# Where a DMA-bound kernel waits for its last store: ahead of the closing barriers, or behind them

## The chip, the cores and the metric

The kernel runs on one core of one Trainium2 chip. Times are device microseconds (us). The state of one core's executions can't be told from a second die, so a run counts as fast unless it lies over 1.5% above the fastest of its kernel; all timed runs here were fast, except one single run whose state is unknown and whose time is not used. PE (matrix products; PEld is its weight loading), ACT, DVE and POOL are the engines that compute; SP here only issues transfers and waits. A semaphore is a counter that instructions raise and wait for; in the traces each of the 23 DMA transfers raises its own by 16 in all, and "landed" here means that the sixteenth increment is there. A barrier is a point at which every engine waits until all have arrived. "Span" is the time from the first to the last instruction of the kernel's own program in the trace.

## The reference

```python
# x: 16 x 2048 x 256 float32;  W: 256 x 256;  rank 16;  scale = 1.0
x_flat = x.reshape(-1, 256)
y = x_flat @ W
lora_out = ((x_flat @ lora_A) * lora_E) @ lora_B
y = y + scale * lora_out        # 16 x 2048 x 256 float32
```

Input and output are 33.5 MB each. The kernel folds the low-rank part into one 256 x 256 weight matrix at the start, so that the rest is one matrix product over 32,768 rows.

## The kernel before

The rows are cut in 8 chunks of 4 MB. A chunk is loaded to SBUF, cast to bf16 by POOL, transposed by PE, copied by ACT, multiplied by PE, copied back over the loaded data by DVE, and stored. SP issues every load and store, in the fixed order below. All of this stands in one "critical block". At its end all engines signal SP once. The last store alone stands behind the block, so that the framework tracks it and waits for it when the kernel closes.

```python
ORDER = [
    "L0", "L1", "L2", "L3", "L4", "L5",
    "S0", "S1", "L6", "L7", "S2", "S3", "S4", "S5", "S6", "S7",
]
# ... (cut)
    stored_of = {c: sem(f"stored_{c}") for c in range(N_CHUNKS - N_HOMES)}   # chunks 0, 1
    stored_rest = sem("stored_rest")                                         # the others
# ... (cut) in the program of SP:
        for step in ORDER[:-1]:
            c = int(step[1:])
            if step[0] == "L":
                # ... (cut) loads
            else:
                sync.wait_ge(s_chunk, c + 1)
                # ... (cut)
                sync.dma_start(out=y_chunks[c], in_=home(c)[:]).then_inc(stored_of.get(c, stored_rest), 16)
# ... (cut)
    with tc.tile_critical(no_gpsimd_drain=True):
        sync_program()
        gpsimd_program()
        scalar_program()
        vector_program()
        tensor_program()

    last = int(ORDER[-1][1:])
    nc.sync.dma_start(out=y_chunks[last], in_=home(last)[:])
```

What the framework adds behind that last line is not in the source, but it is in the built program: SP waits for the last store; then come a drain, a barrier of all five engines, one POOL instruction that clears the kernel's semaphores, and a second barrier.

## Time and profile before

| | before |
|---|---|
| timed | 164.98 us, median of 3 runs (164.93 to 165.04) |
| span of the profiled run | 163.28 us |
| last PSUM copy of DVE ends | 122.27 us |
| last store issued | 122.66 us |
| last store landed (16th increment of its semaphore) | 162.30 us |
| closing work behind the landing | 0.99 us |

From the page of the kernel before: the span; busy time of each engine with its share of the span; the share of DMA by fortieths of the span, in tenths (9 is 90% or more); the queue of loads and stores with packets, MB and its share of 16 engines' span; and the bytes of HBM.

```profile
span 163.3 us, 2148 instructions
...
PE 99.2 (61%) x778; PEld 82.6 (51%) x778; DVE 79.6 (49%) x66; ACT 66.1 (40%) x65; POOL 67.1 (41%) x70
...
DMA  5999999998998998999999999999999999999990
...
q1 hardware_dynamic: 2976, 67.41, 96.8%
...
HBM read 33.85 MB, written 33.56 MB: 413 GB/s over the span
```

No compute engine is busy more than 61%, and the DMA queue 96.8%. The last digit of the DMA row is 0: in the last 4 us (159.2 to 163.3 us) the 16 engines move little. Two things are in there: fifteen of them finish and one is late, still moving bytes until 161.8 us (after 160.25 us the trace has one packet of 32 KB at a time in flight, the last one ending at 161.83 us), and then, for the last 1.45 us, nothing moves at all.

The timeline of the kernel before from 120 us, with start, duration, engine, line and operation; "SPq" is SP's issuing of a DMA:

```profile
119.69 2.57 DVE L181 COPY home<-psum_y 128x1024 f32<-128x1024 f32 x2 [0.24 <-PE psum_y L204]
...
122.66 0.33 SPq L241 DMA_DIRECT2D out_dram<-home  x1
```

The waits of the DMA queue in the kernel before: who waited, for what, us in total, how often, and the longest:

```profile
SPq L130 <- DVEq L185: 42.0, 4, 13.3
...
SPq L272 <- DMA out_dram<-home: 39.3, 1, 39.3
SPq L230 <- DVEq L230: 10.9, 1, 10.9
...
SPq L272 <- PEq L272: 0.7, 2, 0.6
```

Line 272 is the framework's closing code. SP sits there for 39.3 us after the last store is issued. Add 122.66 + 0.33 + 39.3 and you are at 162.3 us, 1 us before the end of the span. That last microsecond is what the change is after. The line of L230 is the wait at the end of the critical block, for DVE's last chunk. The last line is two waits for the other engines in the closing barriers, 0.7 us together.

The printed views leave out semaphore instructions, so here is what the trace records behind the landing, as a list of start (us), engine and instruction. Semaphores 96 and 97 are the two halves of the barrier, 133 is the one that counts the last store.

```
162.296  sixteenth increment of semaphore 133 arrives
162.313  SP    wait for 133 passes
162.372  SP    drain
162.435  SP    arrives at the first barrier
162.588  SP    released (the others by 162.650)
162.679  SP    arrives at the second barrier
162.762  POOL  clears semaphores 99 to 133, 0.225 us
163.099  POOL  has all arrivals of the second barrier
163.219  SP    released (PE, the last, ends at 163.282)
```

The sixteen increments of that last store did not come together: fifteen arrived between 159.38 and 160.59 us, the last at 162.30 us. In the trace, packets of this store follow each other back to back in chains of eight of 32 KB, 1.21 us each, with one of 4 bytes behind the eighth (so in the 11 chains that can be told apart from end to end); there are 16 of these 4-byte packets. The chain that ended last, at 161.83 us, was 1.6 us behind the next (160.24 us). With 16 engines on the page, the author reads a chain as one DMA engine's work and its 4-byte packet as one increment.

### The profile page before, as it was taken

What the parts mean: (1) busy time and instruction counts of PE and PEld (TensorE: products, weight loads), DVE (VectorE), ACT (ScalarE), POOL (GpSimd) and SP (SyncE); (2) the same over time, 40 slices, a digit from 0 to 9 for tenths busy, and PEclk for the clock granted to TensorE, in tenths of its full rate; (3) what the DMA queues carried; (4) which work ended last, traced back from release to release, by engine and by line L of the source; (5) the groups of instructions that cost most, each with busy time, mean ns of one, the idle gap of its engine ahead of it and who ended that gap; (6) DMA issues with size and microseconds to landing.
All of it is one profiled execution on the core that took longest, in us unless ns stands there. A gap on an engine that the chain in (4) does not pass through costs nothing. (4 is left out here: it accounts for less than half of the span.)

```text
span 163.3 us, 2148 instructions
## 1 busy us (share of the span) xinstructions
PE 99.2 (61%) x778; PEld 82.6 (51%) x778; DVE 79.6 (49%) x66; ACT 66.1 (40%) x65; POOL 67.1 (41%) x70
## 2 busy tenths in 40 slices
PE   0399948999999999999930089999960000000000
PEld 0268837888888888888820078888840000000000
DVE  0115861788988888888850025888880000000000
ACT  3044732777767676777720025677720000000000
POOL 1444615777777677777500155677500000000000
PEclk9999995999999999999995557999996555555555
DMA  5999999998998998999999999999999999999990
GB/s 165 411 452 458 393 498 393 409 490 385 466 433 385 490 385 379 417 425 468 409 442 433 409 450 425 427 433 442 417 450 409 450 425 433 442 425 433 450 393 16
DMA packets 2979, 67.43 MB, mean 413 GB/s; under 512 B 528, under 2 KB 544, under 8 KB 672
## 3 DMA queue, kind: packets, MB, share of 16 engines
q1 hardware_dynamic: 2976, 67.41, 96.8%
q14 instruction: 3, 0.02, 0.0%
HBM read 33.85 MB, written 33.56 MB: 413 GB/s over the span
## 5 line engine op out<-in xcount | busy, mean ns | idle before, releaser
L181 DVE COPY home<-psum_y 128x1024 f32<-128x1024 f32 x64 | 78.4, 1225 | 32.8 <-PE psum_y L204 30.0
L151 POOL CAST stage<-home 128x1024 bf16<-128x1024 f32 x64 | 66.4, 1041 | 48.8 <-PE psum_xt L196 24.8
L162 ACT COPY xt<-psum_xt 128x1024 bf16<-128x1024 bf16 x64 | 64.8, 1012 | 52.7 <-PE psum_xt L196 52.7
L204 PE MATMUL psum_y<-weff,xt 128*128 128x256 bf16 x512 | 70.2, 283 | 1.0
L204 PEld LDWEIGHTS psum_y<-weff,xt 128*128 128x128 bf16 x512 | 48.3, 101 | 14.7 <-issue 7.1
L196 PE MATMUL psum_xt<-ident,stage 128*128 128x128 f32 x260 | 42.6, 290 | 14.0 <-PEq L189 14.0
L196 PEld LDWEIGHTS psum_xt<-ident,stage 128*128 128x128 f32 x260 | 33.2, 151 | 16.1 <-issue 15.1
L216 PE MATMUL psum_y<-ident,a_sb 128*16 128x128 f32 x2 | 0.6, 396 | 6.8 <-DMA a_sb<-in_lora_A_dram 6.8
L167 DVE TENSOR_SCALAR ate<-psum_y,e_sb 16x256 f32<-16x256 f32 x1 | 0.5, 471 | 7.5 <-PE psum_y L216 7.5
L216 PEld LDWEIGHTS psum_y<-ident,a_sb 128*16 128x16 f32 x2 | 0.1, 90 | 6.8 <-issue 6.8
L222 PE MATMUL psum_y<-b_sb,ate 16*128 16x256 f32 x4 | 2.1, 666 | 0.0
L177 DVE TENSOR_TENSOR weff<-w_sb,psum_y 128x512 bf16<-128x512 f32 x1 | 0.7, 689 | 2.4 <-PE psum_y L222 2.4
L162 ACT ACT_TABLE_LOAD x1 | 1.3, 1283 | 0.9 <-SPq L230 0.9
L222 PEld LDWEIGHTS psum_y<-b_sb,ate 16*128 16x128 f32 x4 | 1.2, 318 | 0.5 <-issue 0.3
L133 POOL MEMSET ident<- 128x128 f32 x1 | 0.2, 204 | 0.5 <-SPq L230 0.5
L135 POOL TENSOR_SCALAR_AFFINE_SELECT ident<-ident 128x128 f32<-128x128 f32 x1 | 0.3, 293 | 0.2 <-POOL ident L133 0.2
L258 POOL MEMSET const-float32-0.0<- 128x1 f32 x1 | 0.1, 98 | 0.2 <-issue 0.2
L258 POOL MEMSET const-bfloat16-1.0<- 128x1 bf16 x1 | 0.1, 101 | 0.0
L258 POOL MEMSET const-uint8-127<- 128x1 uint8 x1 | 0.1, 101 | 0.0
L258 POOL MEMSET const-float32-1.0<- 128x1 f32 x1 | 0.1, 98 | 0.0
## 6 DMA issues: line engine op xcount, KB each, us to landing
out_dram<-home SPq DMA_DIRECT2D x8, 4096.0 KB, 42.1
home<-in_x_dram SPq DMA_DIRECT2D x7, 4096.0 KB, 19.9
home<-in_x_dram SPq DMA_DIRECT2D x2, 1024.0 KB, 5.3
home<-in_x_dram SPq DMA_DIRECT2D x1, 2048.0 KB, 10.1
w_sb<-in_W_dram SPq DMA_DIRECT2D x1, 256.0 KB, 5.1
a_sb<-in_lora_A_dram SPq DMA_DIRECT2D x1, 16.0 KB, 4.9
e_sb<-in_lora_E_dram SPq DMA_DIRECT2D x1, 0.1 KB, 4.6
b_sb<-in_lora_B_dram SPq DMA_DIRECT2D x1, 16.0 KB, 4.0
```

What stands on the lines that cost most here:

```text
L133: gpsimd.memset(ident[:], 0.0).then_inc(s_ident, 1)
L135: gpsimd.affine_select(out=ident[:], in_=ident[:], compare_op=ALU.not_equal, fill=1.0, base=0, pattern=[[-1, P]], channel_multiplier=1,).t ...
L151: gpsimd.tensor_copy(out=stage[g % NS][:], in_=home(c)[:, b:b + CG, :]).then_inc(s_stage, 1)
L162: scalar.copy(out=xt[g % NX][:], in_=halves).then_inc(s_xt, 1)
L167: vector.tensor_scalar(out=ate[:], in0=psum_y[0][:R, :KT, :P], scalar1=e_sb[:], scalar2=float(scale), op0=ALU.mult, op1=ALU.mult,).then_in ...
L177: vector.tensor_add(out=weff[:], in0=w_sb[:], in1=psum_y[1][:, :KT, :]).then_inc(s_free, NY)
L181: vector.tensor_copy(out=home(c)[:, b:b + CG, :], in_=psum_y[g % NY][:]).then_inc(s_free, 1)
L196: ins = tensor.transpose(psum_xt[i % NT][:, b, :], words[:, b, :], ident[:])
L204: ins = tensor.matmul(psum_y[i % NY][:, b, :], xt[i % NX][:, b, t, :], weff[:, t, :], start=(t == 0), stop=(t == KT - 1),)
L216: ins = tensor.transpose(psum_y[0][:R, t, :P], a_sb[:, t, :], ident[:])
L222: ins = tensor.matmul(psum_y[1][:, t, :], ate[:, t, :], b_sb[:], start=True, stop=True)
L258: nc = _bacc.Bacc("TRN2", target_bir_lowering=False, num_devices=1)
```

## The change

Its intent is to put the closing work under the stores that are still running. The last store is issued within the critical block, as the others are. No store is tracked by the framework any more, so the closing barriers don't wait for any. SP waits for all six open stores (96 increments) in one instruction, added after the framework's closing code. The semaphore must outlive POOL's clearing, which now runs while increments are still coming in. So it is taken from outside the framework's pool, and POOL clears two ranges, one on each side of it (99 to 114 and 116 to 132 in the trace; the stores' semaphore is 115).

```diff
-    stored_rest = sem("stored_rest")
+    stored_rest = nc.alloc_semaphore("stored_rest")
@@
-        for step in ORDER[:-1]:
+        for step in ORDER:
@@
-    last = int(ORDER[-1][1:])
-    nc.sync.dma_start(out=y_chunks[last], in_=home(last)[:])
+    def wait_for_stores(nc):
+        nc.sync.wait_ge(stored_rest, 16 * N_HOMES).then_inc(stored_rest, -16 * N_HOMES)
+
+    nc.at_finalize(wait_for_stores)
```

## The prediction

> **What bounds the kernel now.** The DMA, from end to end. On the page its queue is busy 96.8% of 16 engines' span (413 GB/s, 67.4 MB); PE, the busiest engine, 61%. Compute ends early: the timeline has DVE's last PSUM copy ending at 122.3 us of the 163.3 us span, and from there to about 159 us the windows view shows only DMA, at 426 to 442 GB/s. The trace's semaphore updates show the last four stores landing 9.7 us apart (133.3, 143.0, 152.6, 162.3 us), long after their issues.
>
> **The end of the span.** The last store is issued at 122.66 us (timeline; 0.33 us to issue). SP then waits 39.3 us for its landing (longest wait of the DMA queue, on the kernel's last line), to 162.31 us. Only then come a drain, an all-engine barrier, POOL's clearing of the semaphores (0.225 us) and a second barrier, to 163.28 us: 0.97 us of closing work behind the last byte, serial, on the path that ends last. [...] 15 increments come between 159.38 and 160.59 us, the sixteenth at 162.30 us. One slow engine sets the end; the change doesn't touch it.
>
> **What the change does.**
> 1. The last store moves ahead of the critical block's closing exchange (122.32 to 122.66 us in before), so it is issued about 0.3 us sooner. Worth nothing: stores are queued before it on the same engines.
> 2. The drain, both barriers and the clearing now run at about 122.5 to 123.7 us, under the DMA. POOL clears two ranges instead of one, since the stores' semaphore is kept out: hidden.
> 3. After them stands one SP wait. Such an instruction takes 0.017 us in the trace, so the span should end about 0.03 us after the landing instead of 0.97 us: 0.94 us saved.
> 4. The timed 164.98 us exceeds the span by 1.7 us. The trace shows updates of another semaphore from 163.52 to 164.04 us, after the kernel's end, which I take for the runtime's barrier [...]. Its third update comes 0.205 us after the second, where the opening one has 0.04 us: an engine came late. With four engines there 38 us ahead, it waits for SP alone. I estimate 0 to 0.3 us and count 0.15 us, if the timer covers it.
>
> **Sum.** 164.98 − 0.94 − 0.15 = 163.9 us, 0.7% faster: within 2%. Range 163.4 to 164.3 us. Chances: faster by over 2% 0.02, within 2% 0.96, slower by over 2% 0.02.
>
> **What would show it.** The last store is issued near 122.3 us on the stores' own line, and lands within 0.2 us of 162.3 us as before (1). Barriers and clearing show near 123 us, none after 160 us (2). The queue's last wait is for the stores, on the added line; the span ends within 0.05 us of it (3). The timed median falls by more than the span (4). DMA GB/s and busy times stay.
>
> **What would make it wrong.** The last DMA engine's lag (1.7 us behind the fifteenth) may differ between programs or chips; it enters one to one. The idle engines may fetch their closing instructions during the stores and take DMA time on the slow engine. The timer may leave out the closing barrier, or SP may reach it late: then 0.9 us or less is gained. Over 2% would need 3.3 us, more than everything after the landing.

That the updates from 163.52 to 164.04 us are a barrier of the runtime was the author's reading, and the 0.15 us an estimate from the two gaps (0.205 against 0.04 us). Of the risks: the traces do show packets on an instruction queue, but the three in the span of the kernel before (8 KB and 0.31 us each) came at 62.6, 73.5 and 102.7 us, those of the changed kernel at 59.4, 72.0 and 102.3 us, and none during the last stores.

## The result, and the profile after

| | before | after |
|---|---|---|
| timed, median | 164.95 us (4 runs, 164.81 to 165.04) | 163.59 us (4 runs, 163.36 to 163.85) |
| span of the profiled run | 163.28 us | 162.04 us |
| last store landed | 162.30 us | 162.00 us |
| from landing to end of span | 0.99 us | 0.03 us |
| timed minus span | 1.79 us (mean of 11 runs) | 1.35 us (mean of 4 runs) |

The ratio of the changed kernel to the kernel before is 0.9921, with a 95% interval of 0.9904 to 0.9938. Ratios here are those of fast runs of the same rounds, so they are not quite the ratio of the medians in the tables. The 1.79 us are from the first batch of experiments below, where each run of the kernel before lists its span.

The page of the changed kernel, the same lines as shown of before:

```profile
span 162.0 us, 2150 instructions
...
PE 96.9 (60%) x778; PEld 80.1 (49%) x778; DVE 79.6 (49%) x66; ACT 66.1 (41%) x65; POOL 67.1 (41%) x70
...
DMA  5999898999999997999999999999999999999992
...
q1 hardware_dynamic: 2976, 67.41, 97.5%
...
HBM read 33.85 MB, written 33.56 MB: 416 GB/s over the span
```

The same bytes are moved in the same number of packets. The share rose from 96.8% to 97.5% because the span is shorter. From 124 to 159 us, the stretch in which the stores alone run, the two kernels look the same (first before, then changed; busy time of PE, PEld, DVE, ACT and POOL, granted PE clock, DMA share, GB/s):

```profile
124.00:159.00 35.00, 0.00 (x0) 0.00 (x0) 0.00 (x0) 0.00 (x0) 0.00 (x0) 0.50 1.00 432
```

```profile
124.00:159.00 35.00, 0.00 (x0) 0.00 (x0) 0.00 (x0) 0.00 (x0) 0.00 (x0) 0.50 1.00 431
```

Timeline of the changed kernel from 120 us, then the waits of its DMA queue:

```profile
119.98 1.23 DVE L181 COPY home<-psum_y 128x1024 f32<-128x1024 f32 x1
121.28 0.33 SPq L130 DMA_DIRECT2D out_dram<-home  x1
```

```profile
SPq L130 <- DVEq L185: 50.5, 5, 13.3
...
SPq L238 <- SPq L238: 39.0, 1, 39.0
...
SPq L271 <- PEq L271: 0.9, 2, 0.7
```

The last store is now on line 130 with the others. The wait at the end of the critical block (10.9 us on line 230 before) is gone; line 130 has five waits instead of four, because SP now waits for DVE's last chunk there. The closing barriers (line 271) take 0.9 us. They run from 121.8 to 123.1 us, and nothing of them is left after 160 us. The 39.0 us wait on line 238 is the added one. The view names SP itself as what it waited for. That is an artefact: the instruction also subtracts 96 from the semaphore that it waits on, and this is the update that came last. The real releaser is the store, whose sixteenth increment arrived at 162.005 us; the wait passed at 162.021 us and ended the span at 162.038 us.

### The profile page after: what moved, and what is told of

Same layout as the page of the kernel before. It is cut to its first block, busy times and chain, and to the rows that moved or that the text cites. A ratio compares the mean times of both kernels' runs of the same rounds, so it can differ in the third digit from the quotient of the medians.

```text
span 162.0 us, 2150 instructions
## 1 busy us (share of the span) xinstructions
PE 96.9 (60%) x778; PEld 80.1 (49%) x778; DVE 79.6 (49%) x66; ACT 66.1 (41%) x65; POOL 67.1 (41%) x70
## 3 DMA queue, kind: packets, MB, share of 16 engines
q1 hardware_dynamic: 2976, 67.41, 97.5%
## 5 line engine op out<-in xcount | busy, mean ns | idle before, releaser
L204 PE MATMUL psum_y<-weff,xt 128*128 128x256 bf16 x512 | 68.4, 278 | 0.4
L204 PEld LDWEIGHTS psum_y<-weff,xt 128*128 128x128 bf16 x512 | 47.0, 99 | 14.4 <-issue 6.4
L196 PE MATMUL psum_xt<-ident,stage 128*128 128x128 f32 x260 | 41.1, 283 | 16.0 <-PEq L189 16.0
L196 PEld LDWEIGHTS psum_xt<-ident,stage 128*128 128x128 f32 x260 | 31.9, 147 | 18.1 <-issue 17.2
```

The lines of the kernel that those rows point to most:

```text
L196: ins = tensor.transpose(psum_xt[i % NT][:, b, :], words[:, b, :], ident[:])
L204: ins = tensor.matmul(psum_y[i % NY][:, b, :], xt[i % NX][:, b, t, :], weff[:, t, :], start=(t == 0), stop=(t == KT - 1),)
```

## The experiments

The theory to test, called the closing theory: the gain is the closing work that no longer follows the landing (0.95 us of span), plus a shorter wave of updates afterwards, taken for the runtime's barrier (timed minus span fell by 0.44 us). Rivals: the earlier issue of the last store makes the gain; barriers cost their time wherever they stand; the shorter time behind the span has another cause; the DMA was luckier in the later runs.

Two batches of four were run (r1 and r2 followed), each on one chip with runs of the kernel before beside it. In the first the kernel before took 165.12 us in the median (11 runs), in the second, on another chip, 164.62 us (11 runs). So compare within a batch, or compare ratios. This table has all eight. The landing is that of the one profiled run; "timed − span" is a mean over all timed runs, and is 1.79 us for the kernel before in both batches.

| run | ratio to before (95%) | landing | landing to end of span | timed − span |
|---|---|---|---|---|
| first batch: e0_after_again | 0.9921 (0.9896 to 0.9947) | 161.97 | 0.03 | 1.32 |
| e2_issued_behind_barriers | 0.9914 (0.9888 to 0.9941) | 162.28 | 0.03 | 1.32 |
| e5_barriers_ahead_of_wait | 0.9932 (0.9904 to 0.9961) | 162.99 | 0.03 | 1.34 |
| e6_all_engines_wait | 0.9958 (0.9930 to 0.9986) | 162.11 | 0.18 | 1.82 |
| second batch: e1_issue_moved_only | 1.0027 (1.0011 to 1.0042) | 161.74 | 1.43 | 1.75 |
| e3_issued_20us_later | 0.9925 (0.9911 to 0.9939) | 161.82 | 0.03 | 1.33 |
| e4_barriers_behind_stores | 1.0036 (1.0022 to 1.0051) | 161.77 | 1.30 | 1.79 |
| e7_act_waits | 0.9933 (0.9918 to 0.9947) | 161.83 | 0.04 | 1.46 |

### e0: the changed kernel again

No edit.

> The changed kernel again, as the reference of this batch. Closing theory (the 0.97 us of barriers and semaphore clearing no longer follow the last landing, and the runtime's barrier after the kernel needs only SP): 0.992 of the kernel before, about 163.6 us, with time minus span about 1.35 us against about 1.7 us before. If the first result was luck of the DMA, the ratio comes back nearer 1.

It took 163.69 us in the median of 6 runs, against 165.12 us, with the same ratio as at first. The gain is not luck. What was luck is that the store landed 0.3 us earlier in the first profile of the changed kernel than in that of the kernel before: in the means of all timed runs, listed to 0.1 us, the span of e0, e2, e3 and e7 is 0.81 to 0.89 us shorter than that of the kernel before, and not more than the 0.95 us of closing work. The tenth that is missing is within the noise (standard error 0.11 to 0.17 us).

### e1: only the issue is moved

```diff
-    stored_rest = nc.alloc_semaphore("stored_rest")
+    stored_rest = sem("stored_rest")
+        sync.wait_ge(stored_rest, 16 * N_HOMES)      # at the end of SP's part of the critical block
-    nc.at_finalize(wait_for_stores)                  # and the function with it
```

> The last store is issued inside the critical block as in the change, but SP waits for the stores there, ahead of all closing work. Closing theory: no gain; the critical block's closing exchange (0.40 us in the changed kernel's trace) now also follows the landing, so 0.3 to 0.4 us slower than the kernel before, about 165.3 us. Rival (earlier issue): the gain stays, about 163.6 us.

It took 164.95 us against 164.62 us before. The profile has the store's issue as early as in the changed kernel:

```profile
121.18 0.33 SPq L130 DMA_DIRECT2D out_dram<-home  x1
```

The view of the DMA queue's waits books the wait for it, 40.2 us, on line 106, together with the two waits before the last two loads:

```profile
SPq L106 <- DMA out_dram<-home: 82.1, 3, 40.2
```

So an early issue alone gains nothing, and this half of the change alone even loses: 1.43 us stand behind the landing instead of 0.99 us, because the signals at the end of the critical block now follow the landing too. The ratio of 1.0027 is 0.44 us of 164.62, and 1.43 − 0.99 is 0.44 us.

### e2: the issue moved the other way

```diff
-        for step in ORDER:
+        for step in ORDER[:-1]:
     def wait_for_stores(nc):
+        nc.sync.dma_start(out=y_chunks[last], in_=home(last)[:]).then_inc(stored_rest, 16)
         nc.sync.wait_ge(stored_rest, 16 * N_HOMES).then_inc(stored_rest, -16 * N_HOMES)
```

> The last store is issued behind the closing barriers, about 1.7 us later than in the changed kernel and later than in the kernel before; the final wait stays last. Closing theory: same as the changed kernel, within 0.2 us, since three stores (29 us of DMA) are queued before it. Rival (the gain comes from the earlier issue of the last store): the gain is gone, 165 us or more.

```profile
122.94 0.33 SPq L240 DMA_DIRECT2D out_dram<-home  x1
```

```profile
SPq L241 <- SPq L241: 39.0, 1, 39.0
```

The store is issued later than in the kernel before (122.66 us), and the whole gain is there: 163.57 us, against 163.69 us of the changed kernel in the same batch. The intervals of the two ratios overlap nearly in full.

### e3: the last store issued 20 us later

The sixth chunk's store gets a semaphore of its own, `stored_5`, and the last store is issued only when that one has landed:

```diff
     def wait_for_stores(nc):
+        nc.sync.wait_ge(stored_5, 16).then_inc(stored_5, -16)
+        nc.sync.dma_start(out=y_chunks[last], in_=home(last)[:]).then_inc(stored_rest, 16)
-        nc.sync.wait_ge(stored_rest, 16 * N_HOMES).then_inc(stored_rest, -16 * N_HOMES)
+        nc.sync.wait_ge(stored_rest, 16 * (N_HOMES - 1)).then_inc(stored_rest, -16 * (N_HOMES - 1))
# ... (cut) the new semaphore, its use by the sixth store, and the loop over ORDER[:-1]
```

> The last store is issued only once the sixth chunk's store has landed, near 143 us, some 20 us later than in the change; one whole store is still queued before it. Closing theory: same as the changed kernel within 0.3 us, about 163.6 us. Rival (issue time counts): 165 us or more.

The timeline and the two long waits of this run:

```profile
142.56 0.33 SPq L242 DMA_DIRECT2D out_dram<-home  x1
```

```profile
SPq L241 <- SPq L241: 20.3, 1, 20.3
SPq L243 <- SPq L243: 19.0, 1, 19.0
```

SP slept 20.3 us before the issue and 19.0 us after it, and the ratio is 0.9925. With one 4 MB store still queued (9.7 us of DMA), it didn't matter here that the next was issued 20 us later. The rival of the earlier issue is out.

### e4 and e5: four more barriers, behind the final wait or ahead of it

```diff
     def wait_for_stores(nc):
+        # e5: here
         nc.sync.wait_ge(stored_rest, 16 * N_HOMES).then_inc(stored_rest, -16 * N_HOMES)
+        # e4: here
+        for _ in range(4):
+            nc.all_engine_barrier()
```

> Four all-engine barriers behind the final wait. From the changed kernel's trace one takes about 0.245 us from one arrival of SP to the next, so four take 1.0 us in the span, and all engines end together again (0.35 us in time minus span). Closing theory: about 1.35 us slower than the changed kernel, 164.95 us, the kernel before's time. Rival (what stands behind the landing doesn't matter): 163.6 us.

> Four more all-engine barriers ahead of the final wait. Closing theory: hidden under the stores, same as the changed kernel within 0.2 us. Rival (barriers cost their time wherever they stand): 1 us more, about 164.6 us.

The waits of the DMA queue, first of e4 (barriers behind, on line 240), then of e5 (barriers ahead, on line 239):

```profile
SPq L238 <- SPq L238: 38.1, 1, 38.1
...
SPq L240 <- PEq L240: 0.9, 4, 0.3
```

```profile
SPq L240 <- SPq L240: 37.7, 1, 37.7
...
SPq L239 <- PEq L239: 1.0, 4, 0.3
```

The barriers are the same four, with 0.9 and 1.0 us of waiting in them. Behind the stores they cost all of the gain and more (1.0036). Ahead of the wait they leave 0.03 us from landing to end and the same time behind the span as e0. They were a little dearer than expected: in the trace of e4, SP's arrivals at two of them are 0.33 us apart, not 0.245 us. The run e5 is 0.3 us slower than e0 in the mean of its six runs, so its expectation (within 0.2 us) was missed, but it is far from the 1 us of the rival. Its profile shows where this lay in that run: the landing was at 162.99 us. The sixteenth increment was already 1.45 us behind the fifteenth in the store that landed at 113.8 us (0.94 us in e0), before any of the barriers had run. So the barriers can't have started it; whether they added to it the runs don't tell, and the two ratios' intervals overlap.

### e6 and e7: who comes last to the runtime's barrier

In e6 SP releases the other four engines after its wait, so that all five leave together. In e7 ACT waits in SP's stead.

```diff
         nc.sync.wait_ge(stored_rest, 16 * N_HOMES).then_inc(stored_rest, -16 * N_HOMES)
+        # e6; in e7 the line above has nc.scalar in place of nc.sync, and nothing is added
+        nc.sync.sem_inc(all_stored, 4)
+        for engine in (nc.tensor, nc.scalar, nc.gpsimd, nc.vector):
+            engine.wait_ge(all_stored, 1).then_inc(all_stored, -1)
```

> After the stores SP releases the other four engines, which waited too, so that all five reach the end together as in the kernel before. Closing theory with its runtime part: span about 0.1 us longer than the changed kernel, time minus span back from 1.35 to about 1.7 us, so about 0.45 us slower in all, 164.05 us. Rival (the kernel's own closing work is the whole gain, time minus span differs for another reason): 0.1 us slower at most, and time minus span stays 1.35 us.

> ACT instead of SP waits for the stores, all else as in the change. In the changed kernel's trace four updates of the runtime's semaphore come at 123.3 to 123.6 us, and five after SP's end, so SP looks like the fifth and last of the way out. Closing theory with its runtime part: the same span within 0.1 us, but ACT stands earlier in that chain, so up to 0.2 us more behind the end: 163.6 to 163.8 us. If time minus span were no matter of who comes last, 163.6 us and 1.35 us.

In e6 the span grew by 0.15 us (0.18 against 0.03 us behind the landing), while timed minus span rose from 1.32 to 1.82 us, the kernel before's 1.79. In e7 it is 1.46 us. The ratios of these runs overlap with those of e0 and e3, but timed minus span doesn't: the six runs of e6 have 1.78 to 1.86 us against 1.28 to 1.37 in e0, and those of e7 1.45 to 1.48 against 1.27 to 1.37 in e3. The trace shows why in the updates of one semaphore (number 2), which none of the kernel's instructions in the profile uses. They come in waves of nine: two up to the kernel's first instruction and, in the kernel before, two behind its last. The author takes each wave for a barrier of the runtime (us from the start of the span; the second opening wave and the first closing one of each run):

```
opening  -0.371 -0.336 -0.298 -0.254 -0.231 -0.119 -0.081 -0.046  0.000
before   163.517 163.551 163.756 163.800 163.823 163.923 163.961 163.995 164.042    (span ends 163.282)
changed  123.341 123.375 123.575 123.619 | 162.182 162.225 162.264 162.298 162.346  (span ends 162.038)
e7       123.950 | 162.003 162.042 162.086 162.109 162.208 162.247 162.281 162.327  (span ends 161.864)
e6       162.523 162.557 162.815 162.858 162.881 162.982 163.022 163.056 163.103    (span ends 162.288)
```

The opening and the closing wave have nine updates in nearly the same rhythm; the opening one takes 0.371 us from the first to the ninth. In the changed kernel four updates were made at 123.34 to 123.62 us, when all engines but SP had ended (the last of them at 123.11 us), and only five had to follow SP's end. If ACT is the last one, a single update is made early and eight follow. Together, all nine follow, with a hole before the third (0.205 us in the kernel before, 0.258 us in e6), which looks like an engine arriving late (in e7, where the others had been waiting for 38 us, the third update comes 0.04 us after the second); the trace doesn't name the engine. The timed duration is 0.12 to 0.13 us less than the time from the start of the span to the last update of the second wave in each of the runs with a profile of its own timed execution (for example 163.36 us, and 163.492 us in the trace). So the timed duration follows these updates one to one in these runs; at which instruction the timer stops the traces don't tell.

### r1 and r2: what sets the landing

With the closing work out of the way, the late DMA engine is the largest thing left at the end (1.80 us from the fifteenth to the sixteenth increment in the changed kernel). In r1, on a third chip, the last chunk's store was cut so that one engine, called the sixteenth, would get only 27 of 32 rows. That a store of 120 partitions leaves one engine out was the author's assumption, which no run shows:

```diff
+                    for p0, p1, s, e in ((0, P, 0, 27), (0, 120, 27, ROWS), (120, P, 27, ROWS)):
+                        sync.dma_start(out=y_chunks[c, p0:p1, s:e, :], in_=home(c)[p0:p1, s:e, :]).then_inc(stored_rest, 16)
```

> The changed kernel, with the last chunk's store cut in three: rows 0 to 26 of all 128 partitions, rows 27 to 31 of partitions 0 to 119 [...], and rows 27 to 31 of the last eight [...]. This asks what now sets the end: in every profile the sixteenth increment of the last store comes 1.3 to 2.3 us after the fifteenth. If the late engine is the sixteenth, the one that the 120-partition store leaves out, it does 5/32 of 9.7 us, 1.5 us, less, and the landing moves from about 162.0 to about 160.7 us: 162.3 us timed. If it is another, landing and time stay as they are, 163.6 us, or are up to 0.3 us later.

It failed: 163.82 us against 164.69 us before (4 runs and 7 runs, ratio 0.9948, 0.9926 to 0.9971), with the landing at 162.49 us. This is no better than the changed kernel's 0.9921; the intervals overlap. The DMA packets of its trace tell more: the engine that ended last sent a packet of 27,648 bytes until 160.27 us and then nine of 5,120 bytes. In the trace of the kernel before, a 128-partition transfer has 128 packets, one per partition (1,920 of 32,768 bytes for 15 transfers), so the eight-partition store can have no more than eight of 5,120 bytes. At least one of the nine was thus from the 120-partition store: the late engine was not left out by it, and the sixteenth was a wrong guess. In r2 the last row of 1, 2, 3, 4, 5, 6, 7 and 100 partitions went out as eight small stores with a semaphore each:

```diff
+                    for n in (*range(1, 8), 100):
+                        sync.dma_start(out=y_chunks[c, p:p + n, r, :], in_=home(c)[p:p + n, r, :]).then_inc(stored_last[n], 16)
+                        p += n
```

> A look at which DMA engine is the late one; the time is not the point. Rows 0 to 30 of the last chunk go out over 16 engines, then the last row of 1, 2, 3, 4, 5, 6, 7 and 100 partitions as eight small stores, each with its own semaphore. [...] the store whose semaphore is the first to be complete only at about 162 us names the late engine: n = 1 means the first, n = 7 but not 6 the seventh. [...]

The last landing of each of the eight (us, from the trace's semaphore updates):

```
partitions      1       2       3       4       5       6       7      100
landed     159.35  159.81  160.03  160.21  161.98  162.18  162.37  162.56
```

The step is between 4 and 5 partitions: the last landings of the stores of 1 to 4 partitions are 0.18 to 0.46 us apart, that of 5 is 1.77 us after that of 4. The store of n partitions got one late increment for each of its 1 to 7 partitions, ten for the hundred, and in the store of five the other four had come by 160.38 us. The trace doesn't number the engines. Named as in the expectation, by the smallest store that meets it, the late engine of this run is the fifth. How a store is spread over the engines the runs show only by these counts.

Why this engine falls behind stays open. The lag of the last increment behind the fifteenth is 0.01 to 0.03 us in the changed kernel's loads of x up to 52.6 us. Then it grows, unsteadily, to 0.68 us at the last load (102.7 us), 1.08 and 1.68 us at the next two stores (113.0 and 123.3 us), and is 1.77 to 1.81 us from there to the end. So over half of it arises after the last load has landed, while stores go out and the engines still compute; after the last copy of DVE (121.2 us) it hardly grows. Whether the stores, the computing or something else makes it, no run tells, nor whether the last increment is the same engine's every time. The stores of r2 that missed the late engine were those of 1 to 4 partitions, with up to four late increments. If those are four of the 16 engines, relieving the late one by such stores means that four take rows of the other twelve. The author's estimate from this and the 1.8 us lag is 0.45 us at best (each us taken from the twelve is three on each of the four, so a quarter of the lag), and less than the spread of the runs, so it was not tried.

## Why the prediction was right or wrong

- **The bound was right.** The same bytes in the same packets, and a DMA share of 1.00 from 124 to 159 us in both kernels.
- **Step 1 was right: the earlier issue is worth nothing.** e1 gains nothing with the early issue, e2 and e3 lose nothing with a late one. The time named for it was a little off: the store was issued at 121.28 us, not 122.3, since DVE's last copy ended about 1 us earlier in that run. In e0, e1 and e4 to e7, with the same compute, it was issued at 121.18 to 122.20 us, with no bearing on the end that can be seen.
- **Step 2 was right.** Barriers and both clearings (0.117 and 0.131 us) ran from 121.8 to 123.1 us under the stores. e5 shows that more of the same there leaves the time behind the landing as it is.
- **Step 3 was right, in mechanism and size.** 0.03 us from landing to end instead of 0.99 us. e4 puts barriers back behind the landing and loses the gain.
- **Step 4 was right in mechanism and mis-sized.** The prediction counted 0.15 us "if the timer covers it", with 0 to 0.3 us as its bounds. Timed minus span fell from 1.79 to 1.35 us, 0.44 us, outside these bounds. The prediction priced only the hole before the third update of the wave. In the traces the last update of the first wave comes 0.76 us after the span before and 0.31 us after it in the changed kernel, 0.45 us less: 0.15 us is the hole, 0.21 us the rest of the shorter wave, since four of the nine updates had come by 123.62 us and only five were left (one and eight in e7, none and nine in e6), and 0.09 us its earlier start (0.14 instead of 0.24 us after the span).
- **The sum.** 0.95 + 0.44 is 1.39 us; the medians differ by 1.36 us, the ratio says 1.30 us (0.0079 of 164.95). The prediction had 1.09 us and 163.9 us; measured was 163.59 us, in its range of 163.4 to 164.3 us.
- **The landing is not as steady as was said.** It was to be within 0.2 us of 162.3; it was at 162.00 in the profiled run and between 161.74 and 162.99 us in those of the experiments. Most of this is the lag of the last increment (1.3 to 2.3 us; the fifteenth came at 160.1 to 160.7 us), which the prediction had named among its risks.

## What to carry to other kernels

Where a kernel ends on its DMA, list what stands behind the last landing and move everything that doesn't need the data ahead of the wait: here 0.95 us of barriers and clearing, at no cost that the runs could tell from noise, provided that the semaphore of the wait isn't cleared meanwhile. Let one engine wait alone, and the right one: part of the updates taken for the runtime's own barrier then came early (four of nine with SP, one with ACT), which was worth another 0.44 us with SP waiting and 0.13 us less with ACT (1.46 against 1.33 us of timed minus span). Don't look for the gain in an earlier issue as long as a store is still queued ahead; in e3 the issue came 20 us later at no loss (ratio 0.9925, against 0.9921 with the early issue).
